# HGRN2/FoX trunk: gate after the i projection, modulation closed inside projections, first MLP groups and weight sums reordered

## The chip, the cores and the metric

One core of one Trainium2 chip. The time is device microseconds of one execution; three runs of the kernel before gave 2635.76 to 2638.70 us, median 2637.94.

## What is computed

A two-layer decoder trunk on one sequence of 1024 rows of 1024 features, all float32. Every sub-layer normalises its input and applies a shift and a scale, and multiplies its output by a gate; these come from a conditioning vector c.

```
mod = silu(c) @ ada_w[l] + ada_b[l]                 # six vectors of 1024 per layer, two more for K/V
h = rms_norm(x) * (1 + scale) + shift
# layer 0, HGRN2, 8 heads of 128, chunks of 64 rows
q, f, i, g = split(h @ w_in)
fg = lb + (1 - lb) * sigmoid(f);  k = 1 - fg;  b = cumsum(log(fg)) in a chunk
o = causal(q e^(b-b_mid) . k e^(b_mid-b)) v + (q e^b) state;  state = decay * state + (k e^(b_last-b)) v
x = x + gate1 * ((rms_norm(o) * norm_g * silu(g)) @ w_out)
# layer 1, FoX: softmax attention with forget gates over K/V shared from x after layer 0
# both layers end with an MLP: 5632 channels, causal convolution of width 3, silu(gate) * value
x = x + gate2 * (conv_glu(h @ w_up) @ w_down)
```

## The kernel before

Products run on TensorE (PE) as float32 in three passes over two halves (high and low) of each operand, so that one projection of one head (1024x1024 by 1024x128) is 48 matmuls with 512 columns, on the lines 102, 103 and 104 of a shared helper. The high half of an operand is a copy on ScalarE (ACT, line 83), the low half a subtraction on VectorE (DVE, line 84). The MLP products are done as a fast scheme with fewer block products, which needs sums of blocks; the sums of the down weights (`weight_sums`, 11 pairs of rows of blocks per layer) are made on the chip, written to HBM (`sd`) and read again. A scheduler orders each engine's queue from the written order and its own estimates; the order tables below show what comes out.

**HGRN2** (`hgrn`, from some 70 to 600 us). Per head there are four projections. `forget(h)` makes f and the decays; `rest(h)` makes q, i and g; `scan` makes the scores, the masked copies `st` (line 685) and the chain of states `hg_sv` on DVE (line 707); `outputs` sums two products per block on PE (lines 721 and 727), squares, and scales on DVE to `hg_on` (line 738). `gate(h)` transposes `hg_on` on PE (line 751) and multiplies by norm_g and silu(g). `gate(h)` is handed to `rest(h + 1)` as `before` and is written behind the q projection of the next head. On PE the order is: outputs of head h, q projection of head h + 1, gate of head h, i projection, g projection. Head h + 1's f stands ahead of the outputs.

**Side work.** The 12 modulation vectors that are not needed at the start are spread over the heads as steps: a step loads 128 rows of `ada_w` (512 KB, issued by POOL, three buffers `raw`) and adds them, times silu(c), to an accumulator `acc` of 1024 columns (line 305 for the first of eight steps of a vector, line 307 for the others). Then eight matmuls with a column of ones (line 350) sum `acc` over its partitions: the close of the vector. There is one buffer for `acc`, so the next vector's first step waits for the close on PE. `SIDE = (4, 5, 5)` steps are written behind the q, i and g projections of each head. `ada_step` writes the close at its next call, that is a projection later. The pairs of weight sums of layer 0 are steps of the same list.

**First MLP groups** (`first_groups` in `ffn_up`, once per layer, from 690 and from 1970 us). Two groups of channels, a and b, are multiplied together while their operands are still being made; p1 to p7 are the block products, and `wx`, `y`, `z` PSUM tiles. `first_value` copies p7's PSUM half out and adds it on DVE (line 903); p4 then writes into the other half of the same tile, and `first_value_left` adds that (line 907). The third group's tile takes the place of b's.

**Others.** `column_load` loads small parameters through SP's queue (line 170) and `column_turn` transposes them on PE (line 176); those of the start are in `st_small` and `st_bias`, those of the convolution (`st_ca`, `st_cb`) come in head 0. In `fox` a pair of weight sums of layer 1 (two loads, four DVE operations, two stores) is written ahead of every third of 64 blocks of logits. `ffn_down` loads its first weights when it starts.

Of the kernel before, what the change touches and what calls it, by code (L numbers as in the profile page):

```python
# [48 lines left out]
KLATE = True  # L49
SIDE = (4, 5, 5)  # L50
LATE = 7
# [3 lines left out]
class Trunk:  # L55
# [88 lines left out]
    def setup(self):  # L144
# [21 lines left out]
        def column_load(wp, name, parts):  # L166
            st = wp.tile([P, P], F32, name="st_" + name)
            r = 0
            for p in parts:
                nc.sync.dma_start(st[r:r + p.shape[0], :], p)  # L170
                r += p.shape[0]
            return st, r
# [123 lines left out]
    def ada_plan(self, vectors):  # L296

        def block(key, v, one, k, box):
            def step():
                raw = self.adap.tile([P, D], F32, tag="raw", name="ada_raw", bufs=3)  # L300
                self.nc.gpsimd.dma_start(raw, self.ada_w[key][k * P:(k + 1) * P, v * D:(v + 1) * D])
                c = self.cact[:, k:k + 1]
                if k == 0:
                    box.append(self.adap.tile([P, D], F32, tag="acc", name="acc", bufs=1))
                    self.nc.vector.tensor_scalar(out=box[0], in0=raw, scalar1=c, scalar2=None, op0=ALU.mult)
                else:
                    self.nc.vector.scalar_tensor_tensor(out=box[0], in0=raw, scalar=c, in1=box[0],  # L307
                                                        op0=ALU.mult, op1=ALU.add)
                if k == KT - 1:
                    self.ada_open.append([key, v, one, box[0], 0])  # L310
            return step

        for key, v, one in vectors:
            box = []
            self.ada_todo += [block(key, v, one, k, box) for k in range(KT)]

    def weight_sums(self, l, tiles):

        V, G, down, out = self.nc.vector, self.nc.gpsimd, self.t["ffn_w_down"][l], self.sd[l]

        def pair(i):
            def step():
                e, o = tiles(), tiles()
                for r, raw in ((2 * i, e), (2 * i + 1, o)):
                    G.dma_start(raw, down[r * P:(r + 1) * P, :])
                e1, e2, o1, o2 = e[:, 0:HALF], e[:, HALF:D], o[:, 0:HALF], o[:, HALF:D]
                V.tensor_tensor(out=o2, in0=e2, in1=o2, op=ALU.add)  # L330
                V.tensor_tensor(out=e2, in0=e1, in1=e2, op=ALU.subtract)
                V.tensor_tensor(out=e1, in0=o2, in1=e1, op=ALU.subtract)
                V.tensor_tensor(out=o1, in0=o1, in1=e1, op=ALU.subtract)
                for r, raw in ((2 * i, e), (2 * i + 1, o)):
                    G.dma_start(out[r * P:(r + 1) * P, :], raw)
            return step

        return [pair(i) for i in range(NFF // 2)]

    def ada_step(self, n, psum=None, lag=0):  # L340

        nc = self.nc
        for e in self.ada_open:
            key, v, one, acc, age = e
            e[4] += 1
            if age < lag:
                continue
            ps = (psum or self.aux_tile)()
            for j in range(KT):
                nc.tensor.matmul(ps[:, j:j + 1], acc[:, j * P:(j + 1) * P], self.ones[:, 0:1], start=True, stop=True)  # L350
            s = slice(v * KT, (v + 1) * KT)
            dst, bias = self.mods[key][:, s], self.ada_bias[key][:, s]
            if one:
                nc.vector.scalar_tensor_tensor(out=dst, in0=ps[:, 0:KT], scalar=1.0, in1=bias, op0=ALU.add, op1=ALU.add)
            else:
                nc.vector.tensor_tensor(out=dst, in0=ps[:, 0:KT], in1=bias, op=ALU.add)
        self.ada_open = [e for e in self.ada_open if e[4] <= lag]
        todo, self.ada_todo = self.ada_todo[:n], self.ada_todo[n:]
        for step in todo:
            step()  # L360
# [220 lines left out]
    def hgrn(self, hs):  # L581
# [3 lines left out]
        with self.work("hg") as wp:  # L585
# [51 lines left out]
            def rest(h, a, b, c, d, e, before):  # L637
                pq = self.mm_tile()
                w = self.early.pop(0) if self.early else self.w_cols(w_in, h * P)
                for n in range(2):  # L640
                    self.dense(pq[:, n * HALF:(n + 1) * HALF], w, hs, n)
                q = T("q")
                nc.scalar.activation(q, pq, AF.Silu)
                nc.vector.tensor_tensor(out=e, in0=q, in1=e, op=ALU.mult)
                nc.vector.tensor_tensor(out=q, in0=q, in1=c, op=ALU.mult)
                before()
                self.ada_step(SIDE[0])

# [108 lines left out]
            for h in range(NH):  # L757
# [44 lines left out]
    def ffn_up(self, l, ops):  # L802
# [44 lines left out]
        def do(*products):  # L847
            for steps in zip(*products):
                for f in steps:
                    f()  # L850

        def begin(j, w=None, before=lambda: None):
# [56 lines left out]
        def first_groups():  # L909
# [18 lines left out]
            first_value(a)  # L928
            do(p4(a))
            first_value_left(a)  # L930
# [34 lines left out]
        for j in range(3, NFF + 1):  # L965
# [5 lines left out]
            if j == NFF:  # L971
                self.ahead_op = self.operand(self.hp, self.ahead[0][:, 0:HALF])
            end(s)
            s = following

    def channel_tile(self, k, pool):

        raw = pool.tile([P, 2, HALF], F32R, tag="h", name="graw").bitcast(F32).rearrange("p a s -> p (a s)")
        self.nc.sync.dma_start(raw, self.gd[k * P:(k + 1) * P, :])
        return raw  # L980

    def ffn_down(self, l, gate, ln=None):
# [6 lines left out]
        with self.work("dn", 6) as wp:  # L989
# [3 lines left out]
                    [self.aux_tile() for _ in range(Q)])  # L993

            def weights(src, parity, half):
                rows = src.rearrange("(i e p) m -> e p i m", e=2, p=P)[parity]
                cols = slice(half * HALF, (half + 1) * HALF)

                def load(i):
                    n = min(2, NP - i)  # L1000
                    raw = self.wraw.tile([P, 1024], F32, tag="wraw", name="wraw_t")[:, 0:n * HALF]
                    nc.sync.dma_start(raw.rearrange("p (a b) -> p a b", a=n), rows[:, i:i + n, cols])
                    hl = self.whl.tile([P, 2, 1024], F32R, tag="whl", name="whl_t")
                    self.split(hl[:, 0, 0:n * HALF], hl[:, 1, 0:n * HALF], raw)
                    return [(hl, a * HALF) for a in range(n)]

                return load

# [88 lines left out]

            down, sums = self.t["ffn_w_down"][l], self.sd[l]
# [155 lines left out]
    def fox(self, hs):  # L1254
# [4 lines left out]
        with self.work("fx") as wp:  # L1259
# [118 lines left out]
            head_sig(s)  # L1378
            sums = self.weight_sums(1, lambda: self.x_tile("down_raw")[0])
# [59 lines left out]
    def body(self):  # L1439
# [11 lines left out]
        self.ada_plan([(0, v, v == 4) for v in (2, 3, 4, 5)] + [("kv", v, v == 1) for v in range(2)])  # L1451
        self.ada_todo += self.weight_sums(0, lambda: self.adap.tile([P, D], F32, tag="raw", name="down_raw", bufs=3))
        self.ada_plan([(1, v, v in (1, 4)) for v in range(6)])
# [21 lines left out]
        with self.work("ada") as self.adap:  # L1475
            self.hgrn(h)
            self.ada_step(0)
        mixed(0, t["a_w_out"][0])
# [39 lines left out]
```

## Time and profile before

| | |
|---|---|
| three runs | 2635.76, 2637.94 (median), 2638.70 us |
| profiled execution | 2630.53 us, of which the span is 2628.6 |
| PE busy | 2522.4 us, 96% of the span |
| DVE, ACT, POOL busy | 71%, 46%, 12% |
| TensorE's mean granted clock | 0.985 of full speed |

The span runs from the first to the last instruction; the rest of an execution lies around it. Idle time in front of an instruction is put down to what released it, the last of the things it waited for. The granted clock has two levels, full (1.0) and half (0.5); a mean between them is a stretch with both.

### The profile page before, as it was taken

The numbers are of one execution on the slowest core, as the hardware profiler recorded it, in microseconds if no ns is written. First come the engines' busy times: TensorE is split into PE (matmuls) and PEld (weight loads), VectorE is DVE, ScalarE is ACT, GpSimd is POOL, SyncE is SP. The second block draws the span as 40 slices with busy tenths as digits, with TensorE's granted clock in tenths as the row PEclk, the third lists the DMA queues.
The fourth block names the chain that finished last, engine by engine and source line by source line (L and its number), as shares of the span: only waits on it lengthen the run. The fifth ranks groups of instructions, "written<-read, shape, count | busy, mean of one in ns | idle before, by whom it ended". The sixth has DMA issues, their size and how long they took to land.

```text
span 2628.6 us, 32301 instructions
## 1 busy us (share of the span) xinstructions
PE 2522.4 (96%) x12312; PEld 2077.5 (79%) x12312; DVE 1863.3 (71%) x2703; ACT 1205.8 (46%) x1769; POOL 321.4 (12%) x449
## 2 busy tenths in 40 slices
PE   6999999999999999999999999999998999999999
PEld 5787777778777888878888988888886888887887
DVE  6756765765777878886765367767658777879754
ACT  6432321334544444544645355556545444445442
POOL 2212222211000000000120034433210000000000
PEclk9999998999999999999999999999999999999999
DMA  8625667525122222573343457542421222228423
GB/s 284 200 97 160 214 209 252 187 75 164 37 84 76 80 88 81 178 260 107 125 145 119 150 180 241 186 128 77 152 68 48 80 81 80 81 89 296 140 97 112
DMA packets 298789, 362.10 MB, mean 138 GB/s; under 512 B 13965, under 2 KB 215160, under 8 KB 298634
## 3 DMA queue, kind: packets, MB, share of 16 engines
q1 hardware_dynamic: 272138, 263.55, 30.8%
q0 software_dynamic: 26496, 96.48, 10.6%
q8 instruction: 97, 1.59, 0.2%
q14 instruction: 58, 0.48, 0.1%
HBM read 276.06 MB, written 83.92 MB: 137 GB/s over the span
## 4 chain that ended last, share of the span: by engine, by line
PE 65%; DVE 14%; DMA 9%; issue 7%; ACT 3%; POOL 2%; SPq 0%; POOLq 0%; DVEq 0%; ACTq 0%
PE mm_t L104 11%; PE mm_t L102 11%; PE mm_t L103 11%; PE aux_t L102 10%; PE aux_t L104 10%; PE aux_t L103 10%; DMA ada_raw<-in_ada_w 3%; DVE whl_t L84 2%; DMA wraw_t<-in_ffn_w_up 2%; DVE op_t L84 1%; DMA sd<-down_raw 1%; DVE acc L307 1%; PE aux_t L1347 1%; DMA ada_raw<-in_kv_ada_w 1%; POOL hg_ss L737 1%
## 5 line engine op out<-in xcount | busy, mean ns | idle before, releaser
L84 DVE TENSOR_TENSOR whl_t<-wraw_t,whl_t 128x1024 fp32r<-128x1024 f32 (+1 forms) x332 | 374.4, 1139 | 133.2 <-ACT whl_t L83 130.2
L83 ACT CAST whl_t<-wraw_t 128x1024 fp32r<-128x1024 f32 (+1 forms) x332 | 319.8, 974 | 277.0 <-DVE wraw_t L829 90.0
L102 PE MATMUL mm_t<-op_t,whl_t 128*128 128x512 f32 x968 | 379.8, 393 | 19.9 <-DVE val L903 10.5
L103 PE MATMUL mm_t<-op_t,whl_t 128*128 128x512 f32 x968 | 379.1, 392 | 2.0 <-DVE op_t L84 2.0
L104 PE MATMUL mm_t<-op_t,whl_t 128*128 128x512 f32 x968 | 378.1, 391 | 0.0
L102 PE MATMUL mm_t<-h_t,whl_t 128*128 128x512 f32 x896 | 362.4, 404 | 0.0
L102 PE MATMUL aux_t<-op_t,whl_t 128*128 128x512 f32 x880 | 348.9, 397 | 8.3 <-ACT whl_t L83 5.2
L104 PE MATMUL mm_t<-h_t,whl_t 128*128 128x512 f32 x896 | 356.4, 398 | 0.1
L103 PE MATMUL mm_t<-h_t,whl_t 128*128 128x512 f32 x896 | 355.2, 396 | 0.4 <-DVE h_t L440 0.4
L103 PE MATMUL aux_t<-op_t,whl_t 128*128 128x512 f32 x880 | 343.8, 391 | 1.2 <-DVE op_t L84 1.1
L104 PE MATMUL aux_t<-op_t,whl_t 128*128 128x512 f32 x880 | 342.4, 391 | 2.5 <-DVE whl_t L84 2.4
L102 PEld LDWEIGHTS mm_t<-op_t,whl_t 128*128 128x128 f32 x968 | 182.6, 189 | 65.0 <-DVE val L903 11.3
L103 PEld LDWEIGHTS mm_t<-op_t,whl_t 128*128 128x128 f32 x968 | 182.8, 189 | 41.0 <-DVE op_t L84 4.2
L104 PEld LDWEIGHTS mm_t<-op_t,whl_t 128*128 128x128 f32 x968 | 182.7, 189 | 38.9 <-DVE whl_t L84 0.8
L102 PEld LDWEIGHTS aux_t<-op_t,whl_t 128*128 128x128 f32 x880 | 165.0, 188 | 57.0 <-ACT whl_t L83 17.6
L104 PEld LDWEIGHTS mm_t<-h_t,whl_t 128*128 128x128 f32 x896 | 171.4, 191 | 37.5 <-issue 0.5
L102 PEld LDWEIGHTS mm_t<-h_t,whl_t 128*128 128x128 f32 x896 | 171.4, 191 | 33.2 <-issue 1.2
L103 PEld LDWEIGHTS mm_t<-h_t,whl_t 128*128 128x128 f32 x896 | 171.2, 191 | 33.2 <-DVE h_t L440 0.8
L104 PEld LDWEIGHTS aux_t<-op_t,whl_t 128*128 128x128 f32 x880 | 165.0, 188 | 39.3 <-DVE whl_t L84 4.2
L103 PEld LDWEIGHTS aux_t<-op_t,whl_t 128*128 128x128 f32 x880 | 165.3, 188 | 36.8 <-DVE op_t L84 2.9
L397 POOL TENSOR_TENSOR sqacc<-sqacc,sq 128x512 f32<-128x512 f32 x29 | 44.3, 1529 | 765.4 <-ACT sq L396 765.0
L307 DVE SCALAR_TENSOR_TENSOR acc<-ada_raw,cact,acc 128x1024 f32<-128x1024 f32 x84 | 107.6, 1281 | 39.2 <-DMA ada_raw<-in_ada_w 30.0
(310 smaller groups left out, 4382.7 us busy)
## 6 DMA issues: line engine op xcount, KB each, us to landing
wraw_t<-in_ffn_w_up SPq DMA_DIRECT2D x88, 512.0 KB, 3.7
ada_raw<-in_ada_w POOLq DMA_DIRECT2D x80, 512.0 KB, 4.9
down_raw<-in_ffn_w_down POOLq DMA_DIRECT2D x44, 512.0 KB, 4.7
sd<-down_raw POOLq DMA_DIRECT2D x44, 512.0 KB, 4.1
gd<-u SPq DMA_DIRECT2D x44, 512.0 KB, 2.6
graw<-gd SPq DMA_DIRECT2D x44, 512.0 KB, 6.6
wraw_t<-sd SPq DMA_DIRECT2D x40, 512.0 KB, 3.4
wraw_t<-in_a_w_in SPq DMA_DIRECT2D x32, 512.0 KB, 5.4
```

The lines of the kernel that those rows point to most:

```text
L83: self.nc.scalar.copy(hi, src)
L84: self.nc.vector.tensor_tensor(out=lo, in0=src, in1=hi.bitcast(F32), op=ALU.subtract)
L102: mm(out, wh, xh, start=start, stop=False, skip_group_check=onto)
L103: mm(out, wh, xl, start=False, stop=False, skip_group_check=onto)
L104: mm(out, wl, xh, start=False, stop=stop, skip_group_check=onto)
L307: self.nc.vector.scalar_tensor_tensor(out=box[0], in0=raw, scalar=c, in1=box[0], op0=ALU.mult, op1=ALU.add)
L397: (nc.gpsimd if k in SQPOOL else nc.vector).tensor_tensor(out=self.sqacc[n], in0=self.sqacc[n], in1=sq, op=ALU.add)
L737: nc.gpsimd.tensor_tensor(out=ss[:, s4], in0=ss[:, s4], in1=self.mhalf[:, 0:4], op=ALU.pow)
L1347: nc.tensor.transpose(pp[:, b * P:(b + 1) * P], ls[:, kb * P:(kb + 1) * P], self.ident)
```

## The change

The line numbers of the diff's rows are those of the kernel after, where the close is on line 353, the gate's transposes on line 763, and the two adds of the first groups on lines 921 and 925.

- `gate(h)` is written behind the i projection of head h + 1 instead of the q projection.
- A modulation vector is closed after half of the next projection (`ada_close`) instead of at the next call of `ada_step`; the third burst of steps is written behind the scan; SIDE is (4, 6, 4).
- In the first groups p4 is written ahead of `first_value`, and p5 and p6 of the two groups are interleaved (`skewed`).
- Small column loads are issued by POOL instead of SP.
- `ffn_down`'s first weights are loaded while `ffn_up` ends (`ahead_w`).
- A weight sum is four sub-steps; in `fox` two are written ahead of each block, in heads 0 to 2.

```diff
-SIDE = (4, 5, 5)
+SIDE = (4, 6, 4)
...
-                nc.sync.dma_start(st[r:r + p.shape[0], :], p)
+                nc.gpsimd.dma_start(st[r:r + p.shape[0], :], p)
...
+            def first():
+                for r, raws in ((2 * i, e), (2 * i + 1, o)):
+                    raws.append(tiles())
+                    G.dma_start(raws[0], down[r * P:(r + 1) * P, :])
+                V.tensor_tensor(out=o[0][:, HALF:D], in0=e[0][:, HALF:D], in1=o[0][:, HALF:D], op=ALU.add)
...
+            return [first, minus((e, HALF), (e, 0), (e, HALF)), minus((e, 0), (o, HALF), (e, 0), 2 * i, e),
+                    minus((o, 0), (o, 0), (e, 0), 2 * i + 1, o)]
...
-    def ada_step(self, n, psum=None, lag=0):
+    def ada_close(self):
...
-        for e in self.ada_open:
-            key, v, one, acc, age = e
-            e[4] += 1
-            if age < lag:
-                continue
-            ps = (psum or self.aux_tile)()
+        for key, v, one, acc in self.ada_open:
+            ps = self.aux_tile()
...
-        self.ada_open = [e for e in self.ada_open if e[4] <= lag]
+        self.ada_open = []
+
+    def ada_step(self, n):
...
                 for n in range(2):
                     self.dense(pq[:, n * HALF:(n + 1) * HALF], w, hs, n)
+                    if n == 0:
+                        self.ada_close()
...
-                before()
                 self.ada_step(SIDE[0])
...
                 for n in range(2):
                     self.dense(pi[:, n * HALF:(n + 1) * HALF], w, hs, n)
+                    if n == 0:
+                        self.ada_close()
+                before()
...
                     self.dense(pg[:, n * HALF:(n + 1) * HALF], w, hs, n)
+                    if n == 0:
+                        self.ada_close()
                 sg = T("sg")
                 nc.scalar.activation(sg, pg, AF.Silu)
-                self.ada_step(SIDE[2])
+                self.ada_close()
...
                     self.conv_setup()
+                self.ada_step(SIDE[2])
                 if h < NH - 1:
                     f = forget(h + 1)
...
+            for f in (a[0], b[0], a[1], b[1], a[2], a[3], b[2], b[3]):
+                f()
...
-            do(p5(a), p5(b))
+            skewed(p5(a), p5(b))
...
-            do(p6(a), p6(b))
+            skewed(p6(a), p6(b))
...
             do(p7(a))
+            do(p4(a))
             first_value(a)
-            do(p4(a))
             first_value_left(a)
...
             do(p7(b))
+            do(p4(b))
             first_value(b)
-            do(p4(b))
             first_value_left(b)
...
+                self.ahead_w = self.down_weights(t["ffn_w_down"][l], 0, 0)(0)
...
-                product(x, weights(down, 0, 0), b11, [(0, 0, False)], each=reload(0))
+                first = weights(down, 0, 0)
+                product(x, lambda i: first(i) if i else ahead, b11, [(0, 0, False)], each=reload(0))
...
-                    if (h * KT + i) % 3 == 0 and sums:
-                        sums.pop(0)()
+                    if h < 3 or i < 4:
+                        for f in sums[:2]:
+                            f()
+                        sums = sums[2:]
```

PE, around the gate of the fourth head (`mm_t_2495` is the q projection of the fifth head, `mm_t_2600`, and `mm_t_2587` in the change, its i projection, the next tile its g). Before:

```order
L104 MATMUL mm_t_2495<-h_t_600,whl_t_2498 128x512
L102 MATMUL mm_t_2600<-h_t_368,whl_t_2603 128x512 [waits Activation_49]
...
L104 MATMUL mm_t_2600<-h_t_436,whl_t_2603 128x512
L751 MATMUL aux_t_2554<-ident_100,hg_on_2457 128x128 [waits DVE_49,Activation_49]
...
L104 MATMUL mm_t_2600<-h_t_600,whl_t_2603 128x512
L102 MATMUL mm_t_2671<-h_t_368,whl_t_2674 128x512 [waits Activation_49]
```

And in the change:

```order
L104 MATMUL mm_t_2495<-h_t_600,whl_t_2498 128x512
L102 MATMUL mm_t_2587<-h_t_368,whl_t_2590 128x512 [waits Activation_49]
...
L104 MATMUL mm_t_2587<-h_t_600,whl_t_2590 128x512
L763 MATMUL aux_t_2642<-ident_100,hg_on_2457 128x128 [waits DVE_49,Activation_49]
...
L102 MATMUL mm_t_2674<-h_t_368,whl_t_2677 128x512 [waits Activation_49]
```

The gate stood 9 matmuls into the i projection, 57 behind the outputs; it now stands 96 behind them.

PE, the close of the first vector in the g projection of head 0 (`mm_t_835` before, `mm_t_838` in the change). Before:

```order
L104 MATMUL mm_t_835<-h_t_600,whl_t_838 128x512
L350 MATMUL aux_t_891<-ones_103,acc_752 128x1 [waits DVE_49]
L350 MATMUL aux_t_891<-ones_103,acc_752 128x1 x7
L677 MATMUL aux_t_934<-ident_100,hg_b_677 128x128 x4
```

And in the change:

```order
L104 MATMUL mm_t_838<-h_t_580,whl_t_841 128x512
L353 MATMUL aux_t_868<-ones_103,acc_752 128x1 [waits DVE_49]
L353 MATMUL aux_t_868<-ones_103,acc_752 128x1 x7
L102 MATMUL mm_t_838<-h_t_388,whl_t_841 128x512
```

The close stood behind all 48 matmuls of the projection and now stands behind the first 24.

DVE, the end of the first groups of layer 0 (`val_5168`, and `val_5180` in the change, is group b's value; `whl_t_5201` is the first weight of the third group). Before:

```order
L887 TENSOR_TENSOR u_5145<-u_5145,u_5149 128x1024 [waits DVE_49]
L84 TENSOR_TENSOR whl_t_5113<-wraw_t_5058,whl_t_5113 128x1024 [waits PE_49,Activation_49]
L903 TENSOR_TENSOR val_5168<-mm_t_4863,p5_5013 128x512
L881 SCALAR_TENSOR_TENSOR u_5184<-gate_5055,col_ca0_1012,u_5184 128x1023
L883 SCALAR_TENSOR_TENSOR u_5184<-gate_5055,col_ca0_1012,u_5184 128x1022 [waits DVE_49]
L84 TENSOR_TENSOR whl_t_5201<-wraw_t_5197,whl_t_5201 128x1024 [waits DMAHW5_49,Activation_49]
L826 TENSOR_TENSOR wraw_t_5197<-wraw_t_5197,wraw_t_5198 128x512 [waits DMAHW7_49,DVE_49]
L827 TENSOR_TENSOR wraw_t_5198<-wraw_t_5198 128x512 [waits DVE_49]
L907 TENSOR_TENSOR val_5168<-mm_t_4863,val_5168 128x512 [waits PE_49]
```

And in the change:

```order
L905 TENSOR_TENSOR u_5145<-u_5145,u_5149 128x1024 [waits DVE_49]
L84 TENSOR_TENSOR whl_t_5113<-wraw_t_5058,whl_t_5113 128x1024 [waits Activation_49]
L921 TENSOR_TENSOR val_5180<-mm_t_4863,p5_5013 128x512 [waits Activation_49]
L925 TENSOR_TENSOR val_5180<-mm_t_4863,val_5180 128x512
L899 SCALAR_TENSOR_TENSOR u_5184<-gate_5055,col_ca0_1000,u_5184 128x1023 [waits Activation_49]
L84 TENSOR_TENSOR whl_t_5201<-wraw_t_5197,whl_t_5201 128x1024 [waits DMAHW6_49,Activation_49]
L901 SCALAR_TENSOR_TENSOR u_5184<-gate_5055,col_ca0_1000,u_5184 128x1022 [waits DVE_49]
```

Both adds now stand together where the first one stood, and p4 no longer waits for the first.

## Rows read from the trace of the kernel before

**Rows 1.** The page: span, busy time by engine, chain that ended last.
```profile
span 2628.6 us, 32301 instructions
...
PE 2522.4 (96%) x12312; PEld 2077.5 (79%) x12312; DVE 1863.3 (71%) x2703; ACT 1205.8 (46%) x1769; POOL 321.4 (12%) x449
...
PE 65%; DVE 14%; DMA 9%; issue 7%; ACT 3%; POOL 2%; SPq 0%; POOLq 0%; DVEq 0%; ACTq 0%
```

**Rows 2.** Waits of PE: us in total, times, longest.
```profile
PE aux_t L751 <- DVE hg_on L738: 12.7, 10, 4.8
PE mm_t L102 <- DVE val L903: 10.5, 2, 5.4
PE aux_t L176 <- DMA st_small<-in_q_norm_g: 10.4, 1, 10.4
PE aux_t L350 <- DVE acc L307: 9.3, 4, 3.1
PE aux_t L721 <- DVE hg_sv L707: 5.5, 3, 3.4
...
PE aux_t L102 <- DVE nm L1332: 2.9, 1, 2.9
```

**Rows 3.** Windows behind gates: us; busy PE, PEld, DVE, ACT, POOL; PEclk; DMA; GB/s.
```profile
329.00:332.40 3.40, 3.40 (x12) 2.74 (x12) 2.98 (x4) 0.00 (x0) 0.97 (x2) 0.50 0.94 277
390.40:397.20 6.80, 5.89 (x16) 4.86 (x17) 6.80 (x10) 0.00 (x0) 2.15 (x4) 0.50 0.46 169
```

**Rows 4.** Windows 216.3:223.2, 424.6:431.4, 448.4:451.9, 571.3:574.7 (behind closes); their sum.
```profile
sum 20.60, PE 19.54 PEld 18.38 DVE 10.98 ACT 4.98 POOL 3.44; mean PE 4.88 PEld 4.60 DVE 2.74 ACT 1.24 POOL 0.86
```

**Rows 5.** Windows 468.9:472.3, 523.5:533.8 (behind state waits); last and sum.
```profile
523.50:533.80 10.30, 10.30 (x37) 6.04 (x37) 5.72 (x12) 0.60 (x1) 1.23 (x2) 0.50 0.37 109
sum 13.70, PE 13.70 PEld 8.56 DVE 8.91 ACT 0.60 POOL 1.23; mean PE 6.85 PEld 4.28 DVE 4.46 ACT 0.30 POOL 0.61
```

**Rows 6.** Windows 724.9:731.8, 2008.3:2015.2 (first groups); their sum.
```profile
sum 13.80, PE 8.85 PEld 7.02 DVE 12.06 ACT 5.11 POOL 0.00; mean PE 4.42 PEld 3.51 DVE 6.03 ACT 2.55 POOL 0.00
```

**Rows 7.** Timeline, DVE then PE, fifth gate: start, us, instruction [idle <-releaser].
```profile
388.13 0.69 DVE L330 TENSOR_TENSOR down_raw<-down_raw 128x512 f32<-128x512 f32 x1 [1.16 <-DMA down_raw<-in_ffn_w_down]
...
390.48 0.68 DVE L738 TENSOR_TENSOR hg_on<-aux_t,hg_ss 128x512 f32<-128x512 f32 x1
...
391.31 1.09 PE L751 MATMUL aux_t<-ident,hg_on 128*128 128x128 f32 x4 [4.81 <-DVE hg_on L738]
```

**Rows 8.** Timeline of DVE, accumulation of one modulation vector (eight steps from 199.91).
```profile
199.91 0.75 DVE L305 TENSOR_SCALAR acc<-ada_raw,cact 128x1024 f32<-128x1024 f32 x1 [0.70 <-PE aux_t L350]
...
213.28 1.28 DVE L307 SCALAR_TENSOR_TENSOR acc<-ada_raw,cact,acc 128x1024 f32<-128x1024 f32 x1 [1.98 <-DMA ada_raw<-in_ada_w]
215.54 1.28 DVE L307 SCALAR_TENSOR_TENSOR acc<-ada_raw,cact,acc 128x1024 f32<-128x1024 f32 x1 [0.97 <-DMA ada_raw<-in_ada_w]
```

**Rows 9.** Timeline of PE, then DVE, head 0.
```profile
86.42 0.39 PE L104 MATMUL mm_t<-h_t,whl_t 128*128 128x512 f32 x1
86.65 0.39 PE L102 MATMUL mm_t<-h_t,whl_t 128*128 128x512 f32 x1
...
97.53 1.84 PE L350 MATMUL aux_t<-ones,acc 128*128 128x1 f32 x16
...
94.03 2.59 DVE L307 SCALAR_TENSOR_TENSOR acc<-ada_raw,cact,acc 128x1024 f32<-128x1024 f32 x2
...
105.53 0.72 DVE L685 COPY_PREDICATED st<-mask,aux_t 128x512 f32<-128x512 uint8 x1
```

**Rows 10.** Timeline of DVE, then PE, first groups of the first layer.
```profile
726.95 0.68 DVE L903 TENSOR_TENSOR val<-mm_t,p 128x512 f32<-128x512 f32 x1
...
733.96 0.68 DVE L907 TENSOR_TENSOR val<-mm_t,val 128x512 f32<-128x512 f32 x1
...
727.69 0.79 PE L102 MATMUL mm_t<-op_t,whl_t 128*128 128x512 f32 x1 [5.12 <-DVE val L903]
...
734.70 0.50 PE L102 MATMUL mm_t<-op_t,whl_t 128*128 128x512 f32 x1 [0.95 <-DVE val L907]
```

More of the change, by code (lines that the diff above doesn't have):

```diff
@@ L309, in step @@
                 if k == KT - 1:
-                    self.ada_open.append([key, v, one, box[0], 0])
+                    self.ada_open.append((key, v, one, box[0]))
             return step
@@ L317, in weight_sums, with minus, f @@
     def weight_sums(self, l, tiles):
-        V, G, down, out = self.nc.vector, self.nc.gpsimd, self.t["ffn_w_down"][l], self.sd[l]
+        V, G, down = self.nc.vector, self.nc.gpsimd, self.t["ffn_w_down"][l]
         def pair(i):
[L325 to L336, printed above, removed]
+            e, o = [], []
+            def first():
[3 more added lines that the diff above has]
+                V.tensor_tensor(out=o[0][:, HALF:D], in0=e[0][:, HALF:D], in1=o[0][:, HALF:D], op=ALU.add)
+            def minus(out, a, b, row=None, raws=None):
+                def f():
+                    (t0, c0), (t1, c1), (t2, c2) = out, a, b
+                    V.tensor_tensor(out=t0[0][:, c0:c0 + HALF], in0=t1[0][:, c1:c1 + HALF], in1=t2[0][:, c2:c2 + HALF],
+                                    op=ALU.subtract)
+                    if raws:
+                        G.dma_start(self.sd[l][row * P:(row + 1) * P, :], raws[0])
+                return f
+            return [first, minus((e, HALF), (e, 0), (e, HALF)), minus((e, 0), (o, HALF), (e, 0), 2 * i, e),
+                    minus((o, 0), (o, 0), (e, 0), 2 * i + 1, o)]
         return [pair(i) for i in range(NFF // 2)]
-    def ada_step(self, n, psum=None, lag=0):
+    def ada_close(self):
         nc = self.nc
-        for e in self.ada_open:
-            key, v, one, acc, age = e
-            e[4] += 1
-            if age < lag:
-                continue
-            ps = (psum or self.aux_tile)()
+        for key, v, one, acc in self.ada_open:
+            ps = self.aux_tile()
             for j in range(KT):
@@ L850, in do, with skewed @@
                     f()
+        def skewed(a, b):
+            for f in (a[0], b[0], a[1], b[1], a[2], a[3], b[2], b[3]):
+                f()
         def begin(j, w=None, before=lambda: None):
@@ L980, in channel_tile, with down_weights, load @@
         return raw
+    def down_weights(self, src, parity, half):
+        rows = src.rearrange("(i e p) m -> e p i m", e=2, p=P)[parity]
+        cols = slice(half * HALF, (half + 1) * HALF)
+        def load(i):
+            n = min(2, NFF // 2 - i)
+            raw = self.wraw.tile([P, 1024], F32, tag="wraw", name="wraw_t")[:, 0:n * HALF]
+            self.nc.sync.dma_start(raw.rearrange("p (a b) -> p a b", a=n), rows[:, i:i + n, cols])
+            hl = self.whl.tile([P, 2, 1024], F32R, tag="whl", name="whl_t")
+            self.split(hl[:, 0, 0:n * HALF], hl[:, 1, 0:n * HALF], raw)
+            return [(hl, a * HALF) for a in range(n)]
+        return load
     def ffn_down(self, l, gate, ln=None):
@@ L993, in ffn_down @@
                     [self.aux_tile() for _ in range(Q)])
[L995 to L1007, printed above, removed]
             def minus(out, a, b):
@@ L1096, in outputs @@
                 return f
-            down, sums = self.t["ffn_w_down"][l], self.sd[l]
+            down, sums, weights = self.t["ffn_w_down"][l], self.sd[l], self.down_weights
+            ahead = self.ahead_w
             with self.work("odd", 2 * NP - 15) as self.odd:
                 self.x = [self.x_tile("x_r")[1] for _ in range(KT)]
-                product(x, weights(down, 0, 0), b11, [(0, 0, False)], each=reload(0))
+                first = weights(down, 0, 0)
+                product(x, lambda i: first(i) if i else ahead, b11, [(0, 0, False)], each=reload(0))
                 product(y, weights(down, 1, 0), b21, [(0, 0, True)], each=reload(1))
@@ L1378, in fox @@
             head_sig(s)
-            sums = self.weight_sums(1, lambda: self.x_tile("down_raw")[0])
+            sums = [f for steps in self.weight_sums(1, lambda: self.x_tile("down_raw")[0]) for f in steps]
             for h in range(NH):
@@ L1451, in body @@
         self.ada_plan([(0, v, v == 4) for v in (2, 3, 4, 5)] + [("kv", v, v == 1) for v in range(2)])
-        self.ada_todo += self.weight_sums(0, lambda: self.adap.tile([P, D], F32, tag="raw", name="down_raw", bufs=3))
+        self.ada_todo += [lambda steps=steps: [f() for f in steps] for steps in self.weight_sums(0, lambda: self.adap.tile([P, D], F32, tag="raw", name="down_raw", bufs=3))]
         self.ada_plan([(1, v, v in (1, 4)) for v in range(6)])
@@ L1476, in body @@
             self.hgrn(h)
-            self.ada_step(0)
+            self.ada_step(99)
+            self.ada_close()
         mixed(0, t["a_w_out"][0])
```

## Prediction

> **What bounds the kernel now.** I read the page first. PE is busy for 2522.4 of 2628.6 us, 96%, and PE has 65% of the chain that ended last [rows 1]. So only two things are left to gain on this engine: the time in which it is idle (106 us), and the time in which it is busy at half clock. No engine behind it is full, so what counts is who is late where. The waits of PE, read second, say that [rows 2]. The largest are the gate transposes behind `hg_on` (12.7 us in ten waits), the first groups behind `val` (10.5 in two), the start (10.4), the modulation closes behind `acc` (9.3 in four) and the outputs behind `hg_sv` (5.5 in three). Third, the windows behind these waits: the granted clock is 0.50 for 3.40 us from 329.00, and 0.50 for 6.80 us from 390.40 [rows 3]. Most long waits in HGRN2 and in the first groups are followed by such a stretch, which is the lower of the clock's two levels, 1.2 instead of 2.4 GHz. At that level PE's busy time is twice what the same work takes, so half of the busy time in a stretch is lost as well.
>
> The sum is made against the profiled execution, 2630.53 us. It lies 7.4 us under the median of the runs shown, 2637.94, and the changes are taken over to the median as they are.
>
> **Gates.** Before, the fourth gate stood 57 matmuls behind the outputs, now it stands 96 behind them; the fifth moves further still. One matmul starts every 0.23 us [rows 9], so 39 more give 9 us of cover. The longest wait, 4.81 us, is for an `hg_on` that DVE wrote at 390.48, behind a weight sum that had itself waited for its load [rows 7]. Nine microseconds cover it. Of the 12.7 us [rows 2] I leave 1.5 to the last head, where no projection follows and nothing moves: -11.2. The two windows hold 3.40 + 5.89 = 9.29 us of busy time at half clock [rows 3]: -4.6. Together -15.8. Ends: 0, where DVE is later by as much as PE is earlier, and -17.3.
>
> **Closes.** Gone are the waits of 9.3 us [rows 2], which came from eight steps piling up behind a late close, and half of the 19.54 us in their windows [rows 4]: -9.3 - 9.8 = -19.1. But every close now has half a projection of cover, 24 x 0.23 = 5.5 us, where it had a whole one. A step costs 1.28 us on DVE if its rows have landed; a whole vector at a stretch ran from 199.91 to 216.82, 2.1 us a step, with DVE waiting for `ada_raw` before the last two [rows 8]. With three buffers loaded ahead, the fourth step of a burst ends 3 x 1.28 + 2.1 = 5.9 us after its start, the fifth at 8.0, the sixth at 10.1. By the counts (4, 6, 4) most vectors end early in a burst; four do not. Vector 1 (fourth of its burst) can be read from the trace: its `acc` was done at 94.03 + 2.59 = 96.62 with DVE busy throughout, and its projection began 48 x 0.23 = 10.9 us before the close at 97.53, at 86.6, so that its middle is at 92.1 [rows 9]. The new order has the close there: a wait of 4.5 us. Vector 3 ends as sixth of its burst, but the scheduler put its close behind 33 matmuls, 7.6 us: 2.5. The last ends as fifth: 8.0 - 5.5 = 2.5. Vector 4 as fourth: 0.4. In all 9.9 us, and for the three longer ones a short window as after 329.00, 3.40 us at half clock [rows 3]: 3 x 1.7 = 5.1. Net -19.1 + 15.0 = -4.1. Ends: -19.1, and all twelve closes as vector 1 (a rival, below).
>
> **Outputs.** The third burst no longer stands ahead of the scan, whose state chain shares DVE with it, but behind it. At stake are 5.5 us [rows 2] and half of 13.70 us in two windows [rows 5], 12.4 together. The order still shows steps between the states in the next head, so I take a quarter: -3.1. Ends: 0 and -12.4.
>
> **Head 0.** In the new order six steps of vector 2 stand on DVE ahead of the masked copies that the state products need. The second copy ended at 106.25 [rows 9]. If vector 2 starts at 96.7 and runs at 1.28 and then 2.1 us a step, the copies end at about 109.8, while PE comes 4.5 us later than before because of the wait at vector 1: +1.0 (ends 0 and +5).
>
> **First groups.** Before, p4 of group b waited 5.12 us until 727.69 for the first add, which DVE reached at 726.95, and the third group's first matmul waited 0.95 until 734.70 for the second add at 733.96 [rows 10]. Now p4 can start at 722.57, and its 12 matmuls end at 725.3. Both adds follow at 726.95, to 728.3: the third group's tile is free 6.4 us earlier. Against that, some 4 matmuls that already ran ahead of 734.70 (0.9 us), the low half of the third group's weights, which stands two operations behind the adds (1.2 us, the width of a DVE operation with 1024 columns), and perhaps a short window behind a wait of 3 us (1.7). That gives -2.6 to -4.3, and I take -3.5 a layer, -7.0 in all. Their old windows [rows 6] are inside these spans. Ends -4 and -10.4.
>
> **The rest.** The weight sums of FoX come in smaller pieces and sooner; the largest wait there is 2.9 us behind `nm` [rows 2]. I take -1.5 (ends +2.9 and -4.3). The early load of the down weights and the interleaved p5 and p6 leave PE's and SP's order as good as it was, so they cost nothing and give nothing; the cover is the same queue position. The column loads leave SP's queue for POOL's, which is idle at the start. Today PE's first instruction waits 10.4 us for one of them [rows 2], and the rows of x that it transposes next come out of the same SP queue: 0, with 2 us either way. The Trainium skill (DMA: Bandwidth & Descriptors, "Issuing engine by pattern" and "Specifications") speaks against this edit: it calls the hardware path of SP the faster one for a simple load, with 0.6 us to the first byte where POOL's takes 1. By that rule the sum would be 0.4 us worse; no row here shows either figure.
>
> Sum: -15.8 - 4.1 - 3.1 + 1.0 - 7.0 - 1.5 = -30.5. 2637.94 - 30.5 = **2607.4 us**. About 0.2%, 5.3 us, is what a measurement of this kernel can tell from no change.
>
> **Rivals.**
> - The closes take the place of the waits removed, and the kernel is slower. If all twelve pay what vector 1 pays, 4.5 us and 1.7 of clock, that is 74 us, against gains of 15.8 + 19.1 + 3.1 + 7.0 + 1.5 - 1.0 = 45.5: +29, 2667. It decides from 3.8 us a close on. For it: loads of 512 KB bound the steps [rows 8]. Against: most vectors end as first to third of a burst, and their first steps are loaded ahead. Chance 0.08.
> - DVE is the true pace of HGRN2: what PE gains at one wait it loses at the next, since the same DVE work must be done. Then -5 to +5, about 2637. For it: the gate waited behind unrelated DVE work [rows 7]. Against: DVE is busy for 71% [rows 1]. It also covers the case that the new order, in which parts of the change are not to be seen, does little. Chance 0.10.
> - The clock stays. The waits go, but shorter ones in other places pull the granted clock down as often, and no window is saved. Waits alone: -11.2 - 9.3 + 9.9 - 1.4 + 1.0 - 7.0 - 1.0 = -19, 2619. For it: the wait of 4.81 us is followed by 6.80 us at half clock [rows 3, 7], while of the three state waits, 5.5 us in all with 3.4 for the longest [rows 2], one of the shorter two is followed by 10.30 [rows 5], so length of wait and loss hardly go together. The Trainium skill (TensorE: Matmul & The Clock Gate, "What's actually happening") says the same of the slow stretch, that it varies with the phase in which the chip happens to look, from run to run of one kernel. Chance 0.20.
> - Nothing new appears: all closes are covered and the outputs too. -15.8 - 19.1 - 12.4 - 10.4 - 4.3 = -62, 2576; I count here all below -42. Chance 0.12.
>
> **How the numbers follow.** The forecast, -24 to -42, has 0.50. Faster by over 0.2%: 0.50 + 0.20 + 0.12 = 0.82. Same 0.10, slower 0.08. The range is to hold 8 in 10. Down to 2585 it takes in half of the last rival, up to 2636 the clock rival and half of the case of no gain; outside are 0.06 below and 0.13 above.
>
> **What would show it.** Right: no gate wait over 1 us outside the last head; closes waiting near 90 to 97 us (4.5) and at few other places; the third group's first matmul near 6 us after p4's start; fewer half-clock windows between 110 and 600 us than before. Wrong: waits behind `acc` at most closes or more than 12 us in all; gate waits that only become outputs' or projections' waits behind other DVE rows; first PE instruction later than 11 us.

## The result and the profile after

| | before | the change |
|---|---|---|
| median of the runs | 2638.10 us (4 runs) | 2624.26 us (2617.77 to 2626.53, 4 runs) |
| ratio to before, 95% interval | | 0.9945 (0.9926 to 0.9964) |
| profiled execution / its span | 2630.53 / 2628.6 us | 2626.53 / 2624.8 us |
| mean granted clock, profiled | 0.985 | 0.977 |

The change is faster by 0.55%, about 14 us, where 30.5 were forecast. The waits of PE in the profile after (us in total, times, longest), against [rows 2]:

```profile
PE aux_t L353 <- DVE acc L307: 15.2, 4, 8.3
PE aux_t L710 <- DVE st L697: 13.8, 7, 6.7
PE mm_t L102 <- ACT whl_t L83: 11.6, 4, 5.3
PE aux_t L176 <- DMA st_small<-in_q_norm_g: 10.1, 1, 10.1
...
PE aux_t L733 <- DVE hg_sv L719: 2.7, 2, 2.0
...
PE aux_t L763 <- DVE hg_on L750: 1.3, 2, 0.8
```

The gate's waits are gone as forecast: 12.7 us are 1.3, at the last head. The first groups no longer wait for `val`, and the outputs wait less. But the closes wait 15.2 us instead of 9.3, the state products wait 13.8 us for the masked copies `st`, which before was a small row:

```profile
PE aux_t L698 <- DVE st L685: 2.5, 6, 0.9
```

And the first groups wait for a weight. The clock did not come back either; its mean is lower than before in this execution. HGRN2 from 90 to 600 us, before and after (us; busy time of PE, PEld, DVE, ACT, POOL; clock; DMA share; GB/s), first before:

```profile
90.00:600.00 510.00, 477.91 (x2585) 391.74 (x2585) 341.17 (x449) 164.81 (x189) 104.48 (x165) 0.95 0.52 171
```

and after:

```profile
90.00:600.00 510.00, 476.04 (x2575) 392.31 (x2574) 337.80 (x448) 161.78 (x187) 108.12 (x170) 0.93 0.52 171
```

In the same 510 us PE did ten instructions fewer, and the first MLP product behind HGRN2 starts at 674.91 us instead of 672.96: this stage is no faster in the trace. What DVE waits for there, in the profile after:

```profile
DVE down_raw L331 <- DMA down_raw<-in_ffn_w_down: 41.2, 10, 7.2
DVE acc L307 <- DMA ada_raw<-in_ada_w: 32.4, 29, 4.2
DVE acc L305 <- PE aux_t L353: 18.7, 6, 6.0
```

The first two, with 4.1 us for `in_kv_ada_w`, are loads of the side work, 78 us in all; in the kernel before the same three waits are 25.4, 29.5 and 8.5, 63 us. The longest close is an example; the timeline (start us, us, instruction, idle before and its releaser) of DVE, then POOL, then PE:

```profile
416.51 1.28 DVE L307 SCALAR_TENSOR_TENSOR acc<-ada_raw,cact,acc 128x1024 f32<-128x1024 f32 x1 [4.16 <-DMA ada_raw<-in_ada_w]
...
426.93 1.28 DVE L307 SCALAR_TENSOR_TENSOR acc<-ada_raw,cact,acc 128x1024 f32<-128x1024 f32 x1 [1.06 <-DMA ada_raw<-in_ada_w]
```

```profile
405.98 0.54 POOL L339 DMA_DIRECT2D sd<-down_raw  x1
407.71 0.54 POOL L339 DMA_DIRECT2D sd<-down_raw  x1 [1.19 <-DVE down_raw L336]
411.50 1.06 POOL L301 DMA_DIRECT2D ada_raw<-in_ada_w  x2 [3.26 <-DVE acc L307]
413.98 0.53 POOL L301 DMA_DIRECT2D ada_raw<-in_ada_w  x1 [1.42 <-DMA sd<-down_raw]
...
426.16 0.53 POOL L301 DMA_DIRECT2D ada_raw<-in_ada_w  x1 [2.00 <-DVE acc L307]
```

```profile
428.26 1.01 PE L353 MATMUL aux_t<-ones,acc 128*128 128x1 f32 x4 [8.31 <-DVE acc L307]
```

POOL can issue a load only when one of the three `raw` buffers is free. From 405.98 on two of them hold a weight sum until its stores have landed, so no load is issued until 411.50 (two) and 413.98 (a third); later loads follow DVE's own steps. DVE waits 4.16 us, until 416.51, for the first of these loads and 0.2 to 1.3 us for each of the five behind it, and PE waits for DVE.

### The profile page after: what moved, and what is told of

It is laid out like the page before. It is cut to its first block, busy times and chain, and to the rows that moved or that the text cites. A ratio compares the mean times of both kernels' runs of the same rounds, so it can differ in the third digit from the quotient of the medians.

```text
span 2624.8 us, 32311 instructions
## 1 busy us (share of the span) xinstructions
PE 2529.3 (96%) x12312; PEld 2089.2 (80%) x12312; DVE 1859.0 (71%) x2703; ACT 1204.2 (46%) x1767; POOL 325.0 (12%) x464
## 4 chain that ended last, share of the span: by engine, by line
PE 70%; DVE 11%; DMA 8%; issue 6%; ACT 2%; POOL 1%; SPq 0%; POOLq 0%; DVEq 0%; ACTq 0%
PE mm_t L102 12%; PE mm_t L104 12%; PE mm_t L103 12%; PE aux_t L102 10%; PE aux_t L104 10%; PE aux_t L103 10%; DMA ada_raw<-in_ada_w 3%; DMA wraw_t<-in_ffn_w_up 2%; DVE whl_t L84 2%; DMA sd<-down_raw 1%; PE aux_t L1369 1%; DMA down_raw<-in_ffn_w_down 1%; DVE op_t L84 1%; DVE acc L307 1%; ACT whl_t L83 1%
## 5 line engine op out<-in xcount | busy, mean ns | idle before, releaser
L102 PE MATMUL mm_t<-op_t,whl_t 128*128 128x512 f32 x968 | 379.1, 393 | 15.4 <-ACT whl_t L83 11.6
```

Source lines behind the costliest of these rows:

```text
L102: mm(out, wh, xh, start=start, stop=False, skip_group_check=onto)
```

## The experiments

Each was timed beside the kernel before on its chip; before has medians from 2640.85 to 2643.68 there, so the ratios are compared.

| run | ratio to before | median, us |
|---|---|---|
| e4, f1: the change again | 0.9932 (0.9912 to 0.9953), 0.9946 (0.9931 to 0.9960) | 2623.21, 2627.11 |
| e1: third burst ahead of the scan | 0.9949 (0.9934 to 0.9964) | 2628.34 |
| e2: before + gate move | 1.0001 (0.9988 to 1.0014) | 2642.06 |
| e3: before + p4 first | 0.9967 (0.9954 to 0.9980) | 2632.93 |
| e5: change, gate back | 0.9956 (0.9940 to 0.9973) | 2630.60 |
| e6: change, four buffers | 0.9832 (0.9811 to 0.9854) | 2601.39 |
| e8: change, early weights | 0.9903 (0.9886 to 0.9919) | 2616.73 |
| e9: change, closes late | 0.9942 (0.9924 to 0.9960) | 2627.91 |
| e10: e6 + e8 | 0.9781 (0.9760 to 0.9802) | 2585.12 |
| e11: before, four buffers | 0.9868 (0.9847 to 0.9888) | 2608.71 |
| e12: e11 + gate move | 0.9802 (0.9782 to 0.9822) | 2590.35 |
| e13: small parts undone | 0.9963 (0.9948 to 0.9978) | 2634.11 |
| f2, f3: one small part undone | 0.9958 (0.9943 to 0.9973), 0.9932 (0.9916 to 0.9948) | 2631.71, 2625.45 |
| f4: e10 with before's closes | 0.9749 (0.9733 to 0.9765) | 2576.07 |

**The change again, and the parts alone.** First the unaltered change, on two chips.

> The change once more, unaltered, beside the other three. It shows how far times and half-clock stretches of one kernel differ from run to run. Theory: median 2620 to 2627, waits as in its first profile within 3 us each; if the half-clock stretches are a matter of the run, some stretch of the first profile is missing or another length here though the waits are the same.

> The change unaltered, as the measure for the next two on the same chip. Ratio to before 0.992 to 0.996.

Both agree with the first measurement, at a gain of 5 to 7 thousandths. The gate alone:

```diff
-                before()
                 self.ada_step(SIDE[0])
...
                     self.dense(pi[:, n * HALF:(n + 1) * HALF], w, hs, n)
+                before()
```

> The kernel before with the gate alone moved behind the i projection. Theory (the gate waits are real losses and the move's own gain is kept): waits behind hg_on fall from 12.7 to about 1.3 us and the time falls by 10 to 16 us against before, to 2622 to 2628. Rival (what PE gains at the gates it loses at the next wait for DVE, since the loads of the side work pace it): the waits behind hg_on go as well, but those behind acc, hg_sv and st rise by the same sum and the time stays within 4 us of before.

The rival is right: 1.0001. Its waits:

```profile
PE aux_t L350 <- DVE acc L307: 20.5, 4, 11.7
PE aux_t L698 <- DVE st L685: 11.3, 8, 4.1
```

against 9.3 in [rows 2] and 2.5 above. The gate's own row is now

```profile
PE aux_t L751 <- DVE hg_on L738: 1.2, 2, 0.7
```

Between 90 and 600 us the gate waits fell from 12.7 to 1.2 us, by 11.5, and these two rose by 20.0. (e2 is the edit on the kernel before.) The first groups alone:

```diff
+            do(p4(a))
             first_value(a)
-            do(p4(a))
             first_value_left(a)
```

(the same for b)

> The kernel before with p4 alone moved ahead of the first adds (no interleaving of p5 and p6). Theory (the weights of the third group, loaded late, are the next bound): the waits behind val (10.5 us in two) are gone, a wait of 4 to 6 us in each layer for the first weight of the third group takes their place, and the time falls by 4 to 9 us, to 2629 to 2634. Rival (the weights take back all): within 2 us of before.

0.9967, some 9 us: half of what the whole change gains on the same chip (e4), 60% of what it gains in its two other measurements. The waits for `val` on the first add are gone, and waits for a weight, up to 5.3 us, took their place, as expected.

**Parts of the change undone.** The burst behind the scan, moved back:

```diff
                 nc.scalar.activation(sg, pg, AF.Silu)
                 self.ada_close()
+                self.ada_step(SIDE[2])
...
-                self.ada_step(SIDE[2])
                 if h < NH - 1:
```

> The change with its third burst of steps put back behind the g projection, ahead of the scan; all else as in the change. Theory (the burst behind the scan stands on DVE ahead of the masked copies st and, slow by its loads, makes PE wait 13.8 us for st): these waits fall under 4 us, the time falls by 6 to 14 us against the change, to about 2610 to 2618. Rival one (only the half-clock stretches differ from run to run): time within 4 us of the change. Rival two (DVE's and the loads' work paces HGRN2, wherever the steps stand): the st waits fall, but waits behind hg_sv, acc or others rise by as much, time within 4 us of the change.

My theory fell. The time did not fall (2628.34 beside 2623.21 us on one chip), and the waits for `st` were 17.1 us instead of 13.8:

```profile
PE aux_t L711 <- DVE st L698: 17.1, 9, 6.4
```

The place of the burst is not what makes `st` late. Then the gate and the closes:

```diff
+                before()
                 self.ada_step(SIDE[0])
...
-                before()
                 vt = T("a")
```

> The change with the gate alone put back behind the q projection. Theory (HGRN2 is paced by DVE and the loads of the side work; the gate's own move is worth nothing, as it was in the kernel before): waits behind hg_on come back, those behind acc and st fall by as much, time within 4 us of the change (2619 to 2628 beside a change of 2623). Rival (the gate pays once the closes stand inside the projections): 6 to 14 us slower than the change.

```diff
-                    if n == 0:
-                        self.ada_close()
...
+                self.ada_close()
                 self.ada_step(SIDE[0])
```

(the same at the i projection; behind the g projection a close stands already)

> The change with the closes behind whole projections again (at the next burst of steps), bursts and gate as in the change. Theory (a close halfway waits for its steps, but it also frees acc half a projection earlier, so that the next vector's steps start earlier): PE's waits behind acc fall from 15.2 us or so to under 10 us, DVE's wait of acc L305 for the close (18.7 us) rises, and the time rises by 2 to 8 us. Rival one (the closes halfway only cost): the time falls by 4 us or more. Rival two: no difference, within 3 us.

e5 is slower than the change's three measurements by 1 to 2 thousandths (3 to 6 us), with intervals that overlap: the gate's move is worth a few microseconds at most here, and theory and rival are not told apart. The waits went as the theory says: 6.0 us behind `hg_on`, 21.7 behind `acc`, and 2.0 behind `st` instead of 13.8. e9, at 0.9942, lies among the change's three (0.9932 to 0.9946). Its theory fell: PE still waits 17.2 us behind `acc`, and no time was lost. So the closes halfway are not what makes these waits long; rival two, no difference, fits. The small parts, together (e13) and the first and second hunk singly (f2, f3):

```diff
-                nc.gpsimd.dma_start(st[r:r + p.shape[0], :], p)
+                nc.sync.dma_start(st[r:r + p.shape[0], :], p)
...
-                    if h < 3 or i < 4:
-                        for f in sums[:2]:
+                    if (h * KT + i) % 3 == 0:
+                        for f in sums[:4]:
                             f()
-                        sums = sums[2:]
+                        sums = sums[4:]
...
-                self.ahead_w = self.down_weights(t["ffn_w_down"][l], 0, 0)(0)
```

> The change with its three small parts undone together: small columns on SP's queue again, FoX's weight sums as whole pairs at every third block, no down weights ahead. Forecast of the prediction: 1.5 us slower than the change, within 4 us. Rival: 5 us or more slower, so that what the change gained outside the first groups lies here.

> The change with the small column loads on SP's queue again. If these loads hold up SP's queue in the start and in head 0 (the first projection began 1.8 us later with them, 45.4 instead of 43.6 us): 2 us or more slower than the change, up to 8. As predicted (0, 2 either way): within 3 us.

> The change with FoX's weight sums as whole pairs at every third block. As predicted: 1.5 us slower, within 4. If the pieces are what gains outside the first groups: 5 us or more slower. If the pieces cost (the stretch from the first to the last logits took 313.1 us with pairs, 315.5 with pieces in the profiles): 1 to 3 us faster.

Together 0.9963, whose interval begins just above the change's three ratios (0.9932 to 0.9946); singly 0.9958 and 0.9932 beside 0.9946 on one chip, not told apart. Each of these two costs or gives a few microseconds at most, and the early down weights were not run alone; whether the three give 5 together stays open.

**The loads.**

```diff
-                raw = self.adap.tile([P, D], F32, tag="raw", name="ada_raw", bufs=3)
+                raw = self.adap.tile([P, D], F32, tag="raw", name="ada_raw", bufs=4)
...
-            cmask = wp.tile([P, S], F32, name="cmask")
+            cmask = wp.tile([P, S], mybir.dt.bfloat16, name="cmask")
...
-                sv = wp.tile([P, 16, P], F32, tag="sv", name="hg_sv")
+                sv = wp.tile([P, 15, P], F32, tag="sv", name="hg_sv")
```

(`down_raw` likewise, `mf` shares a buffer, and the indices of `sv` are one lower)

> The change with four buffers raw for the side work's loads instead of three (room is made by a bfloat16 mask for the scan, whose zeros and ones are exact, by 15 instead of 16 state slots and by a mask that shares a buffer; the results do not change). Theory (three buffers let loads and stores of the side work hold DVE up): DVE's waits for ada_raw and down_raw, 36.5 and 41.2 us between 90 and 600 us in the change, fall by a third or more, PE's waits behind acc and st (15.2 and 13.8 us) by half, the time by 6 to 15 us. Rival (DVE's own work or the transport paces it, not the buffers): the same waits within a fifth, time within 4 us of the change.

One more buffer brought 0.9832: 1.0 to 1.1% against the change, 26 to 30 us where 6 to 15 were expected, and more than all its edits. The scan with the smaller mask takes 2283 ns in both, so the mask is not what gains. The other two parts of the edit only make room; they were not run without the fourth buffer. DVE's waits for loads from 90 to 600 us in this run:

```profile
DVE down_raw L331 <- DMA down_raw<-in_ffn_w_down: 27.7, 9, 6.4
...
DVE acc L307 <- DMA ada_raw<-in_ada_w: 12.6, 16, 1.4
```

and PE's:

```profile
PE aux_t L763 <- DVE hg_on L750: 9.6, 4, 7.4
PE aux_t L353 <- DVE acc L307: 6.6, 2, 3.5
PE aux_t L710 <- DVE st L697: 3.8, 3, 1.5
```

Closes and `st` together fell from 29.0 to 10.4 us. The same in the kernel before, without and with the gate's move:

> The kernel before with four raw buffers and nothing else. Theory (the side work's loads, held to three buffers, pace HGRN2 in both kernels): 12 to 25 us faster than before, waits behind acc and hg_sv under half. Rival (the four buffers pay only with the closes inside the projections): within 6 us of before.

> The kernel before with four raw buffers and the gate moved behind the i projection. Theory (the gate's gain was taken back by the loads; with the loads out of the way it is kept): 6 to 16 us faster than four buffers alone. Rival (the gate's gain is taken back by DVE's order in any case): within 4 us of four buffers alone.

This settles the cause: the gate's move is worth nothing with three buffers and is kept with four. Four buffers alone give 1.3% (0.9868), more than expected. With them the gate's move, which was worth nothing, gives 0.9802, another 17 us (0.0066 of 2643.68), close to the 15.8 of the prediction. The largest waits of PE between 90 and 600 us in e11:

```profile
PE aux_t L751 <- DVE hg_on L738: 14.7, 9, 7.8
```

and in e12:

```profile
PE aux_t L751 <- DVE hg_on L738: 7.3, 3, 6.1
PE aux_t L698 <- DVE st L685: 4.7, 5, 1.9
```

A wait behind `acc` is listed in neither. One gate wait of 6.1 us stays in e12; DVE stands there in front of `hg_on` with a weight sum that waited 2.12 us for its load. DVE's wait for `ada_raw` in e11 is

```profile
DVE acc L307 <- DMA ada_raw<-in_ada_w: 11.1, 12, 1.9
```

where the kernel before has 29.5. The first MLP product behind HGRN2 starts at these times in the profiles of the kernel before, e2, e11 and e12:

```profile
672.96 0.39 PE L102 MATMUL mm_t<-op_t,whl_t 128*128 128x512 f32 x1
```

```profile
676.80 0.39 PE L102 MATMUL mm_t<-op_t,whl_t 128*128 128x512 f32 x1
```

```profile
646.82 0.39 PE L102 MATMUL mm_t<-op_t,whl_t 128*128 128x512 f32 x1
```

```profile
629.43 0.39 PE L102 MATMUL mm_t<-op_t,whl_t 128*128 128x512 f32 x1
```

So 17.4 of the 21.2 us by which the two profiled spans of e11 and e12 differ lie ahead of it, where the gate is. All waits of PE from 90 to 600 us add up to 25.0 us in e11 and 15.3 in e12, some 10 us less, and the mean granted clock there rises from 0.97 to 0.99.

**The weights of the first groups, and the best version.**

```diff
-            raws = weight_tiles(2)
+            raws = weight_tiles(2, lambda: self.x_tile("wraw_t")[0])
```

> The change with the two weight tiles of the MLP's group 2 in buffers of the x pool, so that the two weight buffers are free for group 3 while the first groups end. Theory (PE waits 5.3 and 3.9 us there for a weight that is loaded late for want of a buffer): the two waits behind whl_t L83 fall under 1.5 us each, the half-clock stretches after 729 and 2009 us shorten, the time falls by 5 to 11 us to 2612 to 2618. Rival (the next wait, for PSUM read out by the adds on L925, takes over at once): waits of 2 to 4 us behind val and a gain under 4 us.

> The change with four raw buffers and the early weights of the first groups together. If the two act in separate stages, their gains against the change add: 23 and 7 us, so a ratio to the kernel before of 0.978 to 0.982 (2584 to 2594 where before is 2642). If the second only takes what the first had taken, 0.983 as with the buffers alone.

The best version takes e10's edits and those of e9 and e1, with SIDE (4, 5, 5):

```diff
-SIDE = (4, 6, 4)
+SIDE = (4, 5, 5)
...
                 self.ada_close()
+                self.ada_step(SIDE[2])
```

> Four raw buffers, gate behind i, first groups with p4 first and early weights, the small parts of the change; but the closes and the third burst where the kernel before has them, SIDE (4, 5, 5). If the closes inside the projections cost once the loads are out of the way: 5 to 16 us faster than the same with the change's closes (ratio 0.9781), at 0.972 to 0.976. If they gain: slower, at 0.980 or above. Either way this is the version meant to beat both kernels.

With the early weights the change's row of 11.6 us becomes

```profile
PE mm_t L102 <- ACT whl_t L83: 2.5, 2, 1.2
```

at 0.9903, 8 to 11 us against the change's three measurements, as expected. The two gains add (0.9781), and the closes of the kernel before, put back into that, make it faster still: 0.9749 (0.9733 to 0.9765), 2576 us. So with four buffers the closes inside the projections, together with the third burst behind the scan and SIDE, cost some 8 us; which of the three it is was not tested. The two intervals overlap slightly (0.9760 to 0.9765). f4 is 2.5% faster than the kernel before and 1.9% faster than the change.

## Why the prediction was wrong

The direction and the size of the first groups held, the sum did not: 14 us instead of 30.5. Of the prediction's own signs of being right, no gate wait over 1 us outside the last head came; of those of being wrong, more than 12 us behind `acc`.

- **Gates, -15.8: the step that failed.** "Nine microseconds cover it" was right for the wait, which went. What failed is that the time would be kept: alone the move measured 1.0001, 0 us (3.4 either way) instead of -15.8, which is the end that the prediction itself names, "where DVE is later by as much as PE is earlier". The rows used for the closes, steps that wait for `ada_raw` [rows 8], pointed to DVE, and the loads behind it, as the pace of this stage; with PE earlier at the gates, it is earlier at the next close and at the next `st`, and waits there. Shown by e2 (waits moved, time equal) and by e12 (the same edit kept its gain once a fourth buffer was there). The rival "DVE is the true pace" named the place, not the cause: DVE is busy for 412.7 us from 43 us to the first MLP product in the kernel before and for 411.5 in e11, yet e11 gets there 26 us sooner; what DVE waited for was loads that had no buffer.
- **Closes, -4.1.** Vector 1 was read well: a wait of 3.63 us at 95.45 where 4.5 were forecast. In all the closes wait 15.2 us instead of the forecast 9.9, and one wait makes up the difference: 8.31 us, where a step's time of 1.28 or 2.1 us did not hold because a weight sum's stores kept two buffers (405.98 to 413.98 above). The clock did not come back. Undone alone (e9), the edit shows no difference that these runs resolve.
- **Head 0, +1.0.** By the prediction's own numbers the copies come 3.5 us later and PE 4.5, which gives no wait; in the profile after there is none over 0.3 us in head 0 (in f1 one of 1.8). The masked copies are late in later heads, nearly all from 298 us on: 13.8 us in seven waits. The prediction read this queue for one head only. That the burst behind the scan causes it was my first explanation after the result, and e1 refuted it.
- **Outputs, -3.1.** 5.5 became 2.7 us of waits, but in a stage that as a whole gained nothing visible, and not by the step that was forecast: with the burst back ahead of the scan (e1) these waits are 2.8 us.
- **First groups, -7.0.** Alone 0.9967 or -8.7 us (3.4 either way): right in size, in part by luck: in the mechanism it was half right. I expected the wait that remains to be for the PSUM tile read out by the second add; after, that add ends at 729.35, and PE waits on until 731.22 for a weight, whose load could start only when a weight buffer came free. The timeline of the profile after, of DVE, ACT and PE:

```profile
728.67 0.68 DVE L925 TENSOR_TENSOR val<-mm_t,val 128x512 f32<-128x512 f32 x1
```

```profile
730.12 1.04 ACT L83 CAST whl_t<-wraw_t 128x1024 fp32r<-128x1024 f32 x1 [2.08 <-DMA wraw_t<-in_ffn_w_up]
```

```profile
731.22 0.80 PE L102 MATMUL mm_t<-op_t,whl_t 128*128 128x512 f32 x1 [5.29 <-ACT whl_t L83]
```

  What I called the third group's tile is the fourth's (group 3), and so is the weight. e8 shows the load as the cause.
- **The rest, -1.5.** f2 and f3 can't be told from the change, and e13 leaves 5 us open for all three together.

The sum of parts that the runs support is -9 for the first groups and -5 to -9 for all else. Where these lie is open. The profiles show no clear part of it in HGRN2: the first MLP product starts at 674.9, 678.8, 678.7 and 666.5 us in the change (its first profile, e4, f1, and f3, which is the same up to there), at 673.0, 676.8 and 677.4 in the kernel before, e2 and e3. And the profiled execution of the kernel before, 2630.53 us, is faster than every one of its timed runs (lowest 2633.68), so that a comparison of two traces can't find them. My forecast took waits from that one execution as if they were the stage's price.

The rival "the clock stays" came nearest with 2619 us, by luck: it counts the gates' 11.2 us of waits as saved, which e2 measured at nothing.

The Trainium skill (Perfetto Trace Analysis, "Optimization Strategy") says that the same gap repeating on the engine that should be full can mean that there is not enough memory to allocate the next tile, and names the buffer count. The runs agree for the closes and `st`: one more buffer of 512 KB was worth 1.3% in the kernel before, where PE's 9.3 us behind `acc` went (e11), and in the change 29.0 us behind `acc` and `st` became 10.4 (e6). They do not for the ten gate waits of [rows 2]: with four buffers there are still nine, 14.7 us, and it took the order on PE to shorten them (e12).

## What to carry to other kernels

A wait that is removed on the bounding engine pays only if the work that it waits for next isn't paced by something else: look at what the engine behind it (here DVE) waits for in the same stage, and at what lets the next load be issued, before the wait is priced as a gain. Test one edit alone where several are made together; the largest term here was worth nothing alone and 17 us after another limit was lifted. And count the buffers of any stream of loads that runs beside a full engine: here one more cost 4 KB per partition and gave more than every reordering.

## What was not expected of the hardware

The same instructions run at different times from one execution to the next. f1 and f3 are the same up to FoX, and the first MLP product after HGRN2 starts at these times, first f1, then f3:

```profile
678.67 0.39 PE L102 MATMUL mm_t<-op_t,whl_t 128*128 128x512 f32 x1
```

```profile
666.50 0.39 PE L102 MATMUL mm_t<-op_t,whl_t 128*128 128x512 f32 x1
```

12 us apart, almost as much as the change gains. PE's waits behind `acc` and `st` ahead of it are 18.7 and 18.3 us in f1, 13.5 and 14.9 in f3, which is 9 of the 12. The timed runs are spread as well: by 8 to 17 us in the edited kernels with three buffers, by 3 to 13 in those with four. The mean granted clock is 0.992 in the profiles of e12 and f4 against 0.977 to 0.982 in the three of the change.
